# Weight sums of the FFN up-projection: bound on VectorE behind the subtraction two places ahead in the plan, where it was one

## The chip, the core and the metric

One core of a Trainium2 chip runs one inference step of a hybrid streaming encoder layer. The metric is the device time of one execution in microseconds (us).

## The reference

Two request groups share the weights: 256 prompt frames and 8 streams of 16 frames, together 384 rows of 2048. The part of the layer that the change touches is the feed-forward network at its end:

```python
h2 = rmsnorm(x, norm_ffn_g)
up = h2 @ w_up                          # 2048 x 11264: gate half, then up half, 5632 columns each
g_half = up[..., :D_FF]
u_half = up[..., D_FF:]
gc = causal_dwconv(concat([ffn_buf, g_half]), ffn_dw_w, ffn_dw_b)
x = x + (silu(gc) * u_half) @ w_down
```

Before it stand the combined input projection, the conformer convolution, the forgetting attention and the output projections, all in float32.

## The kernel before

Every weight goes to TensorE as a pair of halves. A DMA brings a tile of 2 x 128 rows by 512 columns (512 KB) into a slot; ScalarE (ACT) casts it to `hi` (L170), VectorE (DVE) subtracts `hi` from it to get `lo` (L171), and TensorE (PE) makes three matmuls for each product: `hi` with the high half of the activations, `lo` with that half, `hi` with their low half (L1180 to L1182 in the up-projection, L322 to L324 elsewhere). In the feed-forward part there are three pairs of `hi` and `lo`, used in turn, so the cast for a unit can only begin once TensorE is through with the unit three places ahead of it. The raw slots are seven, used in turn.

The feed-forward part is walked in eleven groups of 512 gate and 512 up columns, 0 to 10; after every second group the down-projection of those groups follows (after 8, of 8, 9 and 10). TensorE's order is fixed by hand. For a part of the 2048 rows (two quarters `q`; three of them in groups 3, 5, 7 and 9) the up-projection saves products by a scheme of Strassen's kind: it multiplies not only blocks of the weights but sums of blocks. For one quarter there are four blocks: `b11` and `b21` (gate columns, upper and lower rows) and `b12` and `b22` (up columns). The units, in TensorE's order, with the number of matmuls that read each:

| unit | weight that is split | VectorE's work on it | matmuls |
|---|---|---|---|
| b22 | the block itself | subtraction | 12 |
| t3 | `sums` = b22 + b12 | add, subtraction | 12 |
| t1 | b12 = b12 + b11, in its slot | add, subtraction | 6 |
| b11 | the block itself | subtraction | 12 |
| t2 | `sums` += b11 | add, subtraction | 6 |
| b21 | the block itself | subtraction | 12 |
| t4 | `sums` += b21 | add, subtraction | 6 |

The units `pu` and `pg` of the other quarters are plain blocks with 18 matmuls each. In a group with two mixed quarters one or more `pu` follow each `t1` or the last `t2`; in groups 3, 5, 7 and 9 the second and third quarter follow each other with no plain unit between them (b22 t3 t1 b11 t2, b22 t3 t1 b11 t2).

`planned_mixed` puts one function for each unit into `plan`; `ahead` calls them up to three units before TensorE needs them. A function loads what it needs, makes the add (L203, `add_to`) and then calls `split`, which records the cast and the subtraction. On VectorE and ScalarE a scheduler orders the instructions; the code binds some of them by an edge that sets an order on one engine and waits for nothing (`behind`). An add is bound behind the subtraction of the unit that was split last. Beside this work VectorE evacuates products (L1232 to L1261), turns blocks (L337), and makes the taps and products of the small convolution (L1151 to L1161).

Of the kernel before, what the change touches and what calls it, by code (L numbers as in the profile page):

```python
# [11 lines left out]
ALU = mybir.AluOpType  # L12
# [36 lines left out]
def hybrid_step(  # L49
# [41 lines left out]
    def f(ap):  # L91
        return ap.bitcast(F32)
# [3 lines left out]
    tt = nc.vector.tensor_tensor  # L96
# [8 lines left out]
    newest = {}  # L105

    def behind(d, name):
        tc.add_manual_dep(d.ins, name, mybir.DependencyInfo(
            mybir.DependencyClass.NoSync, mybir.DependencyReason.DATA), reason="queue")
# [35 lines left out]
    def fetch(srcs, by_row=False):  # L145
        slot = slots.pop(0)
        slots.append(slot)
        raw = wp.tile([P, 2, 512], F32, tag="raw", bufs=3, name="raw") if slot is None else slot
        o = 0
        for s in srcs:  # L150
            n = s.shape[-1]
            for k in ((0, 1), (1, 2)) if by_row else ((0, 2),):
                d = nc.sync.dma_start(raw[:, k[0]:k[1], o:o + n], s[:, k[0]:k[1], :])
                queued(d, len(plan) >= v_last)
            o += n
        return raw, o

    depth, ffn = [2], [False]
    pairs_more, splits = [], [0]

    def split(raw, o, by_row=False):
        n = splits[0] % depth[0] - 2
        splits[0] += 1
        if n >= 0:
            hi, lo = pairs_more[n]
        else:
            hi = wp.tile([P, 2, 512], F32R, tag="hi", bufs=2, name="hi")
            lo = wp.tile([P, 2, 512], F32R, tag="lo", bufs=2, name="lo")
        for k in (slice(0, 1), slice(1, 2)) if by_row else (slice(0, 2),):
            nc.scalar.copy(hi[:, k, :o], raw[:, k, :o])  # L170
            newest["lo"] = tt(lo[:, k, :o], raw[:, k, :o], f(hi[:, k, :o]), op=ALU.subtract).ins.name  # L171
        return hi, lo

    plan = []
# [1 line left out]
    def rows_of(w, k, c, n):  # L176
        return w[0, k * P:(k + 2) * P, c:c + n].rearrange("(k p) n -> p k n", p=P)
# [8 lines left out]
    def steps(g):  # L186
        mixed = mixed_of(g)
        pu, pg = ([(f"p{side}{h}", q) for q in range(4) if q not in mixed for h in range(2)] for side in "ug")
        n = len(pu) // 2 if g else 0
        top, low = [], []  # L190
        for i, q in enumerate(mixed):
            top += [(what, q) for what in ("b22", "t3", "t1")] + pu[i:min(i + 1, n)]
            top += [(what, q) for what in ("b11", "t2")]
            low += [[("b21", q), ("t4", q)]]
        if len(mixed) == 2:
            return top + pu[n:] + pg[:1] + low[0] + pg[1:2] + low[1] + pg[2:]
        return top + pu[n:] + low[0] + pg[:1] + low[1] + low[2] + pg[1:]

    def planned_mixed(w, c1, c2, g):
        held = {}  # L200

        def add_to(dst, a, b):
            behind(tt(dst, a, b, op=ALU.add), newest["lo"])  # L203

        def load(rows):
            return fetch([rows])[0]

        def add(fn):
            plan.append(lambda: split(fn(), 512))

        def single(name, k, c):
            held[name] = load(rows_of(w, k, c, 512))
            return held[name]

        def both(q):
            sums[q] = new_sum[0](q)
            add_to(sums[q], held["b22"][:], single("b12", 4 * q, c2)[:])
            return sums[q]

        def across(q):  # L220
            b = held["b12"][:]
            add_to(b, b, single("b11", 4 * q, c1)[:])
            return b

        def grown(q, name):
            add_to(sums[q], sums[q], held[name][:])
            return sums[q]

        make = {"b22": lambda q: single("b22", 4 * q + 2, c2), "t3": both, "t1": across,
                "b11": lambda q: held["b11"], "t2": lambda q: grown(q, "b11"),  # L230
                "b21": lambda q: single("b21", 4 * q + 2, c1), "t4": lambda q: grown(q, "b21")}
        for what, q in steps(g):
            if what[0] == "p":
                k, c = 4 * q + 2 * int(what[2]), {"u": c2, "g": c1}[what[1]]
                add(lambda k=k, c=c: load(rows_of(w, k, c, 512)))
            else:
                add(lambda what=what, q=q: make[what](q))
# [38 lines left out]
    def ahead(n):  # L276
        while plan and len(ready) < n:
            with tc.high_priority(offset=SPLIT_AHEAD):
                if x_left and (len(plan) - v_last) in range(3, 14, 2):
                    load_x(x_left.pop(0), 2)  # L280
                item = plan.pop(0)
                ready.append(item() if callable(item) else split(*fetch(item)))
# [80 lines left out]
    def natural(ap):  # L363
        return ap.rearrange("p (t i c) -> p i t c", t=NTT, i=4)
# [30 lines left out]
    with tc.manual_schedule(engines={ENG.SP, ENG.Activation, ENG.DVE}):  # L395
        nc.vector.memset(junk[:, 0:1], 0.0)
        nc.scalar.activation(junk[:, 1:2], junk[:, 0:1], AF.Identity)
        load_x(0, 1, nc.scalar)
        load_x(1, 1, nc.scalar)
        raws = [fetch(plan.pop(0), by_row=True)]  # L400
        raws.append(fetch(plan.pop(0)))
        load_x(2, 2)
        nc.scalar.dma_start(gm_row[:], norm_mix_g[0].rearrange("(c p) -> c p", p=P))
        warm = misc_tile()
        for i in range(WARM):
            mm(warm[:, :P], ident[:], ident[:], start=True, stop=True)
        pv = misc_tile()
        tr(pv[:, :16], gm_row[:], ident[:16, :16])
        nc.vector.tensor_copy(gm[:], pv[:, :16])
        x_chunk(0)  # L410
        for i in range(WARM_MID):
            mm(warm[:, :P], ident[:], ident[:], start=True, stop=True)
        x_chunk(1)
        for i in range(WARM_END):
            mm(warm[:, :P], ident[:], ident[:], start=True, stop=True)
        ready.append(split(*raws[0], by_row=True))
        ready.append(split(*raws[1]))
# [347 lines left out]
    def load_v(h):  # L765
# [14 lines left out]
                  k=kv[h // 4][:, :, :, h % 4, :]) for h in range(H)]  # L780
# [100 lines left out]
    for h in range(H):  # L881
        v = heads[h]["q"]
        hi, lo = (natural(aHL[h // 4][:, i, h % 4, :]) for i in range(2))
# [473 lines left out]
```

## Time and profile before

| | |
|---|---|
| median of 3 runs | 1980.43 us (1979.89 to 1980.8) |
| profiled execution: time, span | 1980.97 us, 1979.3 us |
| granted TensorE clock | 1.00 in every stretch |
| PE, PEld, DVE, ACT, POOL busy share | 99%, 83%, 66%, 45%, 13% |
| feed-forward part, from about | 910 us to the end |
| a period of two groups and their down-projection | 192.5 us |

Busy times are sums over instructions. A matmul of 512 columns has a record of 0.39 us, but the next begins 0.23 us after it, so TensorE loses more than its idle time shows when it has to wait: the record of the one before covers part of the wait.

### The profile page before, as it was taken

The page shows a single profiled execution, that of the slowest core. Times are in us where ns is not written, and L with a number is a line of the kernel's source. Part 1 is how long each engine was busy: PE and PEld are TensorE (multiplying, and loading weights), DVE is VectorE, ACT ScalarE, POOL GpSimd, SP SyncE. Part 2 cuts the span into 40 slices and gives each one's busy share as a digit, 9 for nine tenths or more (in the row PEclk, how much of TensorE's full clock was granted, in tenths as well). Part 3 has the DMA queues.
Part 4 walks back from the last instruction along what each step waited for, and adds up shares of the span by engine and source line. Part 5 has one row for each costly group of instructions (what it writes and reads, how often), then busy time and mean ns, then how long its engine had stood idle before and what let it go on. Part 6 is the DMA issues. An engine that isn't in the chain of part 4 may idle for free.

```text
span 1979.3 us, 24793 instructions
## 1 busy us (share of the span) xinstructions
PE 1957.6 (99%) x9230; PEld 1643.3 (83%) x9230; DVE 1301.2 (66%) x1715; ACT 898.6 (45%) x1310; POOL 260.0 (13%) x525
## 2 busy tenths in 40 slices
PE   9999999999999999999999999999999999999999
PEld 9999878888888888887888887888788878887887
DVE  4478889747465447457688648854885588558853
ACT  5433343555334423445455444553454345444541
POOL 1001121100000002011112200220022012201210
PEclk9999999999999999999999999999999999999999
DMA  6565776665344448767655675566567655756463
GB/s 185 157 170 161 225 238 201 203 186 156 114 131 122 128 133 273 236 210 233 200 168 180 203 181 154 183 209 169 162 190 207 167 176 181 209 149 191 157 232 113
DMA packets 194901, 358.21 MB, mean 181 GB/s; under 512 B 16386, under 2 KB 66557, under 8 KB 194771
## 3 DMA queue, kind: packets, MB, share of 16 engines
q1 hardware_dynamic: 172779, 272.78, 44.4%
q0 software_dynamic: 21680, 83.70, 15.2%
q8 instruction: 72, 1.18, 0.2%
q14 instruction: 50, 0.41, 0.1%
q10 hardware_dynamic: 320, 0.14, 0.0%
HBM read 301.78 MB, written 55.24 MB: 180 GB/s over the span
## 4 chain that ended last, share of the span: by engine, by line
PE 45%; DVE 3%; ACT 1%; issue 1%; POOL 0%; ACTq 0%; DVEq 0%
PE acc L1181 7%; PE acc L1182 6%; PE acc L1180 6%; PE acc L322 6%; PE acc L324 6%; PE acc L323 6%; PE misc L1181 2%; PE misc L1182 2%; PE misc L1180 2%; DVE lo L171 2%; ACT hi L170 1%; PE misc L322 1%; PE misc L324 1%; PE misc L323 1%; DVE rest L1233 0%
## 5 line engine op out<-in xcount | busy, mean ns | idle before, releaser
L171 DVE TENSOR_TENSOR lo<-raw,hi 128x1024 fp32r<-128x1024 f32 (+2 forms) x345 | 413.2, 1199 | 406.2 <-ACT hi L170 405.7
L170 ACT CAST hi<-raw 128x1024 fp32r<-128x1024 f32 (+2 forms) x345 | 354.6, 1030 | 605.9 <-PE acc L324 418.5
L322 PE MATMUL acc<-hi,hT 128*128 128x512 f32 (+1 forms) x704 | 270.4, 384 | 0.1
L323 PE MATMUL acc<-lo,hT 128*128 128x512 f32 (+1 forms) x704 | 266.1, 378 | 1.5 <-DVE lo L171 1.4
L324 PE MATMUL acc<-hi,hT 128*128 128x512 f32 (+1 forms) x704 | 265.6, 377 | 0.0
L171 DVE TENSOR_TENSOR lo<-rest,hi 128x1024 fp32r<-128x1024 f32 x136 | 165.3, 1221 | 110.2 <-ACT hi L170 109.7
L170 ACT CAST hi<-rest 128x1024 fp32r<-128x1024 f32 x136 | 142.0, 1048 | 125.8 <-PE acc L324 38.2
L322 PE MATMUL acc<-hi,act 128*128 128x512 f32 x484 | 188.3, 389 | 0.0
L323 PE MATMUL acc<-lo,act 128*128 128x512 f32 x484 | 188.3, 389 | 0.0
L324 PE MATMUL acc<-hi,act 128*128 128x512 f32 x484 | 188.3, 389 | 0.0
L323 PEld LDWEIGHTS acc<-lo,hT 128*128 128x128 f32 x704 | 132.3, 188 | 25.7 <-DVE lo L171 4.6
L588 DVE SCALAR_TENSOR_TENSOR ut<-ext,cw,ut 128x384 f32<-128x384 f32 x240 | 149.6, 623 | 5.5
L322 PEld LDWEIGHTS acc<-hi,hT 128*128 128x128 f32 x704 | 132.2, 188 | 24.1 <-issue 1.8
L324 PEld LDWEIGHTS acc<-hi,hT 128*128 128x128 f32 x704 | 132.2, 188 | 22.6
L1181 PE MATMUL acc<-lo,xg 128*128 128x512 f32 x384 | 149.6, 389 | 0.8 <-DVE lo L171 0.8
L1180 PE MATMUL acc<-hi,xg 128*128 128x512 f32 x384 | 149.5, 389 | 0.0
L1182 PE MATMUL acc<-hi,xg 128*128 128x512 f32 x384 | 149.4, 389 | 0.0
L170 ACT CAST hi<-sums 128x1024 fp32r<-128x1024 f32 x78 | 81.9, 1050 | 146.7 <-DVE sums L203 122.6
L1181 PE MATMUL acc<-lo,xm 128*128 128x512 f32 x340 | 134.6, 396 | 9.3 <-DVE lo L171 9.2
L1182 PE MATMUL acc<-hi,xm 128*128 128x512 f32 x340 | 132.4, 390 | 0.0
L1180 PE MATMUL acc<-hi,xm 128*128 128x512 f32 x340 | 132.4, 389 | 0.0
L342 POOL DMA_DIRECT2D turn<-block x124 | 69.2, 565 | 479.2 <-DVE block L337 470.4
(358 smaller groups left out, 3666.2 us busy)
## 6 DMA issues: line engine op xcount, KB each, us to landing
rest<-in_w_up_dram SPq DMA_DIRECT2D x97, 512.0 KB
raw<-in_w_in_dram SPq DMA_DIRECT2D x96, 512.0 KB
raw<-in_w_up_dram SPq DMA_DIRECT2D x79, 512.0 KB
raw<-in_w_down_dram SPq DMA_DIRECT2D x49, 512.0 KB
turn<-block POOLq DMA_DIRECT2D x120, 192.0 KB, 4.6
block<-turn POOLq DMA_DIRECT2D x30, 768.0 KB, 6.2
rest<-in_w_down_dram SPq DMA_DIRECT2D x39, 512.0 KB
raw<-in_w_in_dram SPq DMA_DIRECT2D x64, 256.0 KB
```

Source lines behind the costliest of these rows:

```text
L170: nc.scalar.copy(hi[:, k, :o], raw[:, k, :o])
L171: newest["lo"] = tt(lo[:, k, :o], raw[:, k, :o], f(hi[:, k, :o]), op=ALU.subtract).ins.name
L322: mm(o, ah[:, s], hi[:, kk, :n], start=st, stop=False)
L323: mm(o, ah[:, s], lo[:, kk, :n], start=False, stop=False)
L324: mm(o, al[:, s], hi[:, kk, :n], start=False, stop=sp)
L342: nc.gpsimd.dma_start(d[:, :, i, :].rearrange("j r n -> r j n"), src[32 * i:32 * i + 32, :].rearrange("r (j n) -> r j n", j=4))
L588: stt(o, v, wc, o, op0=ALU.mult, op1=ALU.add)
L1180: mm(o, ah, hi[:, kk, :], start=st, stop=False)
L1181: mm(o, ah, lo[:, kk, :], start=False, stop=False)
L1182: mm(o, al, hi[:, kk, :], start=False, stop=last[b] == (i, n))
```

## The change

The name of every subtraction is kept in a list in the order of the plan, and an add is bound behind the last but one of them instead of the last. Nothing else is edited.

```diff
-    pairs_more, splits = [], [0]
+    pairs_more, splits, halves = [], [0], []
...
-            newest["lo"] = tt(lo[:, k, :o], raw[:, k, :o], f(hi[:, k, :o]), op=ALU.subtract).ins.name
+            halves.append(tt(lo[:, k, :o], raw[:, k, :o], f(hi[:, k, :o]), op=ALU.subtract).ins.name)
...
         def add_to(dst, a, b):
-            behind(tt(dst, a, b, op=ALU.add), newest["lo"])
+            behind(tt(dst, a, b, op=ALU.add), halves[-2])
```

What the scheduler makes of it is shown by the order of the instructions in the two builds. TensorE's order is the same in both. Before the feed-forward part nothing moves on any engine. In it, VectorE, ScalarE, GpSimd and the DMA queue of SyncE are reordered; the number of instructions stays.

First place: VectorE in group 5, from the plain block b22 of the second quarter to the sum t1 of the third. `rest3_7742` in the first rows of the third quarter is its b22, `raw_11126` its b12 and `raw_11139` its b11; `rest2_7741` is the second quarter's b11. Before:

```order
L171 TENSOR_TENSOR lo3_6749<-sums_7738,hi3_6748 128x1024
L203 TENSOR_TENSOR rest1_7740<-rest1_7740,rest2_7741 128x1024
L171 TENSOR_TENSOR lo_11069<-rest1_7740,hi_11068 128x1024
L171 TENSOR_TENSOR lo_11085<-rest2_7741,hi_11084 128x1024
L203 TENSOR_TENSOR sums_7738<-sums_7738,rest2_7741 128x1024
L171 TENSOR_TENSOR lo_11111<-rest3_7742,hi_11110 128x1024
L171 TENSOR_TENSOR lo3_6749<-sums_7738,hi3_6748 128x1024
L203 TENSOR_TENSOR sums_7738<-rest3_7742,raw_11126 128x1024
L171 TENSOR_TENSOR lo_11130<-sums_7738,hi_11129 128x1024
L203 TENSOR_TENSOR raw_11126<-raw_11126,raw_11139 128x1024
L171 TENSOR_TENSOR lo_11157<-raw_11139,hi_11156 128x1024
L171 TENSOR_TENSOR lo3_6749<-raw_11126,hi3_6748 128x1024
```

After:

```order
L203 TENSOR_TENSOR rest1_7740<-rest1_7740,rest2_7741 128x1024
L171 TENSOR_TENSOR lo3_6749<-sums_7738,hi3_6748 128x1024
L171 TENSOR_TENSOR lo_11069<-rest1_7740,hi_11068 128x1024
L203 TENSOR_TENSOR sums_7738<-sums_7738,rest2_7741 128x1024
L171 TENSOR_TENSOR lo_11085<-rest2_7741,hi_11084 128x1024
L171 TENSOR_TENSOR lo3_6749<-sums_7738,hi3_6748 128x1024
L203 TENSOR_TENSOR sums_7738<-rest3_7742,raw_11126 128x1024
L171 TENSOR_TENSOR lo_11111<-rest3_7742,hi_11110 128x1024
L203 TENSOR_TENSOR raw_11126<-raw_11126,raw_11139 128x1024
L171 TENSOR_TENSOR lo_11130<-sums_7738,hi_11129 128x1024
L171 TENSOR_TENSOR lo3_6749<-raw_11126,hi3_6748 128x1024
```

Each add stands one subtraction earlier, and the subtractions now stand in TensorE's order: before, b22 of the third quarter stood ahead of t2 of the second, and b11 ahead of t1. ScalarE's casts are swapped back in the same way at these two spots.

Second place: VectorE in group 6 (two mixed quarters), around t1 of the second quarter (`rest3_7742`) and the plain unit that follows it in TensorE's order (`raw_11530`). Before:

```order
L203 TENSOR_TENSOR sums_7738<-rest2_7741,rest3_7742 128x1024
L171 TENSOR_TENSOR lo_11496<-sums_7738,hi_11495 128x1024
L203 TENSOR_TENSOR rest3_7742<-rest3_7742,raw_11506 128x1024
L171 TENSOR_TENSOR lo3_6749<-raw_11530,hi3_6748 128x1024
L171 TENSOR_TENSOR lo_11510<-rest3_7742,hi_11509 128x1024
L171 TENSOR_TENSOR lo_11552<-raw_11506,hi_11551 128x1024
```

After, where the row of the quarter's b22 (`rest2_7741`) now stands between the two adds:

```order
L203 TENSOR_TENSOR sums_7738<-rest2_7741,rest3_7742 128x1024
L171 TENSOR_TENSOR lo3_6749<-rest2_7741,hi3_6748 128x1024
L203 TENSOR_TENSOR rest3_7742<-rest3_7742,raw_11506 128x1024
L171 TENSOR_TENSOR lo_11496<-sums_7738,hi_11495 128x1024
L171 TENSOR_TENSOR lo_11510<-rest3_7742,hi_11509 128x1024
L171 TENSOR_TENSOR lo3_6749<-raw_11530,hi3_6748 128x1024
```

The subtraction of t1 moved ahead of that of the plain unit, and its add ahead of t3's subtraction. Groups 2, 4, 8 and 10 read alike.

Third place: VectorE in group 5, around t4 of the first quarter (the add of `rest0_7739` to `sums_7738`) and six instructions that evacuate products (L1232 to L1241). Before:

```order
L171 TENSOR_TENSOR lo_11203<-rest0_7739,hi_11202 128x1024
L1232 TENSOR_TENSOR rest0_7739<-misc_11059,rest0_7739 128x512
L203 TENSOR_TENSOR sums_7738<-sums_7738,rest0_7739 128x1024
L1233 SCALAR_TENSOR_TENSOR rest1_7740<-rest0_7739,nr2_6763,rest1_7740 128x512
L1236 SCALAR_TENSOR_TENSOR block_11214<-acc_11005,nr2_6763,rest1_7740 128x512
L1237 SCALAR_TENSOR_TENSOR block_11214<-acc_11005,nr2_6763,block_11214 128x512
L1244 SCALAR_TENSOR_TENSOR block_11214<-acc_11020,r2_6762,block_11214 128x512
L1241 SCALAR_TENSOR_TENSOR block_11214<-acc_10970,r2_6762,block_11214 128x512
L171 TENSOR_TENSOR lo_11220<-sums_7738,hi_11219 128x1024
```

After:

```order
L203 TENSOR_TENSOR sums_7738<-sums_7738,rest0_7739 128x1024
L171 TENSOR_TENSOR lo_11203<-rest0_7739,hi_11202 128x1024
L1232 TENSOR_TENSOR rest0_7739<-misc_11059,rest0_7739 128x512
L171 TENSOR_TENSOR lo_11220<-sums_7738,hi_11219 128x1024
L1233 SCALAR_TENSOR_TENSOR rest1_7740<-rest0_7739,nr2_6763,rest1_7740 128x512
L1236 SCALAR_TENSOR_TENSOR block_11214<-acc_11005,nr2_6763,rest1_7740 128x512
L1237 SCALAR_TENSOR_TENSOR block_11214<-acc_11005,nr2_6763,block_11214 128x512
L1244 SCALAR_TENSOR_TENSOR block_11214<-acc_11020,r2_6762,block_11214 128x512
L1241 SCALAR_TENSOR_TENSOR block_11214<-acc_10970,r2_6762,block_11214 128x512
```

The add went ahead of b21's subtraction, and t4's own subtraction ahead of five of the six evacuations.

## The prediction

> **What bounds the kernel now.** I read the page's first part, then who waited for whom on TensorE, then engine by engine the places where TensorE waits.
>
> ```profile
> PE 1957.6 (99%) x9230; PEld 1643.3 (83%) x9230; DVE 1301.2 (66%) x1715; ACT 898.6 (45%) x1310; POOL 260.0 (13%) x525
> ```
> ```profile
> PE acc L1181 <- DVE lo L171: 10.0, 16, 1.5
> PE misc L1181 <- DVE lo L171: 2.3, 4, 0.6
> ```
>
> TensorE is the bound, and its end is the kernel's end. All that a change on VectorE can give is TensorE's waiting. In the feed-forward part that is 12.3 us of idle time in 20 waits, all of them of L1181, the matmul with `lo`, for its subtraction. A wait costs more than its idle time. TensorE around the start of t2 of group 5's second quarter:
>
> ```profile
> 1388.90 0.39 PE L1182 MATMUL misc<-hi,xm 128*128 128x512 f32 x1
> 1389.12 0.39 PE L1180 MATMUL misc<-hi,xm 128*128 128x512 f32 x1
> 1390.09 0.50 PE L1181 MATMUL misc<-lo,xm 128*128 128x512 f32 x1 [0.58 <-DVE lo L171]
> 1390.43 0.40 PE L1182 MATMUL misc<-hi,xm 128*128 128x512 f32 x1
> ```
>
> The usual step is 0.23 us (1388.90 to 1389.12; 12 matmuls 2.71, 6 of them 1.35, 18 of them 4.06). Here it is 0.97, and the next one 0.34: lost are 0.74 + 0.11 = 0.85 us, the idle time and 0.27 more. So 20 waits lose 12.3 + 20 x 0.27 = 17.7 us. That is the most to be had, 0.9% of the time.
>
> The same view for the stretch from 883 to 1020 us (groups 0 and 1):
>
> ```profile
> PE acc L1181 <- DVE lo L171: 3.1, 3, 1.5
> ```
>
> These three lose 3.9 us. The other 17 have 12.3 - 3.1 = 9.2 us of idle time and lose 13.8 us: one in each of the five even groups from 2 on, three in each of 3, 5, 7 and 9.
>
> VectorE is the late one though it is busy for only 66%. Its subtractions wait for ScalarE's casts, and casts of sums wait for the adds:
>
> ```profile
> DVE lo L171 <- ACT hi L170: 568.9, 326, 4.9
> ACT hi L170 <- DVE sums L203: 122.6, 58, 2.9
> ```
>
> **The change, place by place.** No instruction is added or removed; 104 adds of 1.22 us move. First, group 5, before t2 of the second quarter, VectorE and then ScalarE:
>
> ```profile
> 1377.89 1.22 DVE L203 TENSOR_TENSOR sums<-rest,rest 128x1024 f32<-128x1024 f32 x1
> 1380.30 1.23 DVE L171 TENSOR_TENSOR lo<-sums,hi 128x1024 fp32r<-128x1024 f32 x1 [1.19 <-ACT hi L170]
> 1381.45 1.22 DVE L203 TENSOR_TENSOR rest<-rest,rest 128x1024 f32<-128x1024 f32 x1
> 1383.86 2.36 DVE L171 TENSOR_TENSOR lo<-rest,hi 128x1024 fp32r<-128x1024 f32 x2 [1.19 <-ACT hi L170]
> 1386.13 1.22 DVE L203 TENSOR_TENSOR sums<-sums,rest 128x1024 f32<-128x1024 f32 x1
> 1387.67 1.23 DVE L171 TENSOR_TENSOR lo<-rest,hi 128x1024 fp32r<-128x1024 f32 x1 [0.32 <-ACT hi L170]
> 1388.82 1.22 DVE L171 TENSOR_TENSOR lo<-sums,hi 128x1024 fp32r<-128x1024 f32 x1
> 1389.95 1.22 DVE L203 TENSOR_TENSOR sums<-rest,raw 128x1024 f32<-128x1024 f32 x1
> ```
> ```profile
> 1382.78 2.00 ACT L170 CAST hi<-rest 128x1024 fp32r<-128x1024 f32 x2 [2.50 <-DVE rest L203]
> 1386.59 1.05 ACT L170 CAST hi<-rest 128x1024 fp32r<-128x1024 f32 x1 [1.82 <-PE acc L1182]
> 1387.55 1.05 ACT L170 CAST hi<-sums 128x1024 fp32r<-128x1024 f32 x1
> ```
>
> Each sum goes through add, cast, subtraction with VectorE idle for 1.19 us during the cast, 3.5 us in a row, three times a quarter. Instructions on VectorE start 1.14 us apart when nothing holds them. Where no plain unit of 4.06 us stands between, TensorE (10.8 us a quarter) is faster than that chain (adds of t3 at 1377.89 and 1389.95: 12.1 us). t2's matmuls begin at 1389.12 and want its subtraction one step later, 1389.35; it is done at 1390.04. Its cast had also stood behind one of the next quarter, which waited until 1386.59 for its pair. Counted back by the units' lengths, b11 began at 1386.4 (its own `lo` wanted at 1386.63), t1 at 1385.0, t3 at 1382.3.
>
> With the new order: t1's add fills the idle 1.19 us ahead of 1380.30; its subtraction follows t3's, at 1381.45 instead of 1383.86. Then t2's add, 1382.6 to 1383.8; b11's subtraction, whose pair is free at 1382.3 and cast by 1383.5, 1383.75 to 1385.0 (it was done at 1386.22); t2's cast when its pair is free, with t3's last matmul, 1385.0 to 1386.05; t2's subtraction done at 1387.3, 2 us early.
>
> The second wait there is t1 of the third quarter (chain of waits):
>
> ```profile
> 1394.36 1.06 ACT hi L170
> 1395.45 2.37 DVE lo L171 x2
> 1397.86 0.50 PE acc L1181
> ```
>
> b11's subtraction goes first and t1's second. On from above: t3's add 1387.2, b22's subtraction 1388.35, t1's add 1389.5, t3's subtraction 1390.6 (cast from 1389.2, when its pair is free), t1's cast 1390.75, subtraction 1391.85 to 1393.1. Without the first wait TensorE wants it at 1389.12 + 1.35 + 2.71 + 2.71 + 0.23 = 1396.1. Both waits go.
>
> Third, t4 of the first quarter:
>
> ```profile
> 1403.14 1.23 DVE L171 TENSOR_TENSOR lo<-rest,hi 128x1024 fp32r<-128x1024 f32 x1 [0.65 <-ACT hi L170]
> 1406.02 0.74 DVE L1233 SCALAR_TENSOR_TENSOR rest<-rest,nr,rest 128x512 f32<-128x512 f32 x1
> 1407.47 0.74 DVE L1237 SCALAR_TENSOR_TENSOR block<-acc,nr,block 128x512 f32<-128x512 f32 x1
> 1408.78 0.74 DVE L1241 SCALAR_TENSOR_TENSOR block<-acc,r,block 128x512 f32<-128x512 f32 x1
> 1409.44 1.22 DVE L171 TENSOR_TENSOR lo<-sums,hi 128x1024 fp32r<-128x1024 f32 x1
> 1410.71 0.50 PE L1181 MATMUL acc<-lo,xm 128*128 128x512 f32 x1 [0.30 <-DVE lo L171]
> ```
>
> The five evacuations from 1406.02 to 1409.5 stood ahead of its subtraction. Now it goes ahead of them, and they begin one subtraction (1.14 us) later but without the add (1.13) that was ahead. Without the two waits before, TensorE ends the third quarter at 1389.12 + 12.2 = 1401.3; b21's subtraction is then done at about 1402.3, L1232 at 1402.9, t4's at 1404.1 (wanted 6.8 us after 1401.3), the five evacuations of 0.7 us at 1407.5, and the next plain unit's subtraction at 1408.7, wanted at 1401.3 + 4.06 + 2.71 + 1.35 + 0.23 = 1409.65: 0.9 us to spare. The PSUM bank that t4 writes is free when L1237 is done, 1406.1, also in time. The wait goes.
>
> Fourth, group 6's t1 (VectorE, and TensorE's wait):
>
> ```profile
> 1444.06 1.23 DVE L171 TENSOR_TENSOR lo<-sums,hi 128x1024 fp32r<-128x1024 f32 x1 [1.19 <-ACT hi L170]
> 1447.31 1.23 DVE L171 TENSOR_TENSOR lo<-raw,hi 128x1024 fp32r<-128x1024 f32 x1 [0.89 <-ACT hi L170]
> 1448.45 1.22 DVE L171 TENSOR_TENSOR lo<-rest,hi 128x1024 fp32r<-128x1024 f32 x1
> 1449.72 0.50 PE L1181 MATMUL acc<-lo,xm 128*128 128x512 f32 x1 [0.64 <-DVE lo L171]
> ```
>
> Its add now runs in the 1.19 us ahead of 1444.06, its subtraction at 1445.2 to 1446.4, wanted at 1448.9. The plain unit keeps its 1447.31.
>
> So all 17 repeating waits go: **-13.8 us**.
>
> Groups 0 and 1 are crowded with the evacuation of the output projection:
>
> ```profile
> 910.58 1.23 DVE L171 TENSOR_TENSOR lo<-raw,hi 128x1024 fp32r<-128x1024 f32 x1 [0.90 <-ACT hi L170]
> 911.72 1.22 DVE L203 TENSOR_TENSOR sums<-raw 128x1024 f32<-128x1024 f32 x1
> 912.86 1.88 DVE L1058 TENSOR_TENSOR y<-acc,y 128x512 f32<-128x512 f32 x3
> 914.70 1.22 DVE L171 TENSOR_TENSOR lo<-sums,hi 128x1024 fp32r<-128x1024 f32 x1
> 917.61 2.32 DVE L171 TENSOR_TENSOR lo<-raw,hi 128x1024 fp32r<-128x1024 f32 x2
> ```
>
> After, t1's add, two evacuations and t1's subtraction stand between 911.7 and t3's subtraction: 1.14 + 2 x 0.6 + 1.14 = 3.5, so it begins at 915.2 instead of 914.70 and may miss its matmul by 0.2 us, by 1 if t1's rows land late. Bounds for these three waits: nothing saved to 3.9. I take 1 us left: **-2.9 us**.
>
> What may be late next: an add now holds a subtraction behind it, and in the even groups one tap of the small convolution stands ahead of t2's. The trace has no such order. Bounds: nothing, where VectorE idles 1.19 us (as at 1380.30), to one wait of 0.85 us in each group, 9.4 us. I take 0.5, near the lower end, since the places above have 0.9 us and more to spare: **+0.5 us**.
>
> GpSimd's queue and SyncE's are reordered too. Rows of weights are issued as slots come free, and an add that runs earlier frees its slot earlier; I cost that at nothing.
>
> Sum: -13.8 - 2.9 + 0.5 = -16.2 us, from 1980.97 us of the profiled execution to 1964.8. That run stands 0.54 us above the median, so the median goes from 1980.43 to **1964.2 us**.
>
> **Rivals.**
>
> *The ring of three pairs is the limit.* The casts that begin the late stretches waited for TensorE (1386.59 above, 1394.36, both behind L1182), and an earlier add frees no pair. [...] Against: t2's own pair was free at 1385.0, 2.5 us before its cast began. If it holds, only groups 0 and 1 gain: 1980.4 - 2.9 = 1977.5 us.
>
> *Half.* The swapped subtractions (t2, t1) come right, but the evacuations or the taps, now elsewhere between them, make new waits of the old size in half of the places: 1980.4 - 8.1 = 1972.3 us.
>
> *Slower: adds hold up plain blocks.* If t1's subtraction stayed at 1383.86, t2's add would push b11's from 1386.22 to 1387.36, 0.73 us behind TensorE's 1386.63, in place of a wait that had 0.41 to spare. At 0.73 each, 24 such places eat the 17.7 us; t2 and t4 have 52. With all of them and nothing gained on the way: 1980.4 - 17.7 + 52 x 0.73 = 2000 us. Against: t1's chain moves too.
>
> **How the numbers follow.** The sum as it stands, 1962 to 1966.5: 0.68. Half (1966.5 to 1975.5): 0.18. The ring, or no effect: 0.08. Slower: 0.06. The runs before spread by 0.9 us, so 0.2% (4 us) is about what can be told from no change. Faster by more than that: 0.68 + 0.18 + 0.01 of the ring's upper end = 0.87; within: 0.07; slower: 0.06. The likeliest case's own range is 1962 to 1966.5; 1962 is all 17.7 us and a little. The range for 8 in 10 reaches up through most of the half: 1961.8 to 1972.
>
> **What would show it.** TensorE's waits for `lo` in the feed-forward part fall from 20 to under 5; no wait at t2, t1 and t4 of groups 3, 5, 7 and 9; VectorE's idle time behind ScalarE's casts falls, while its busy time stays near 1301 us; TensorE's busy time stays near 1958 us. A period of 192.5 us becomes 189.3 (four waits of 0.85, 0.91, 0.57, 0.91 less). Waits at b11 or at plain units in their place would show the slower rival, unchanged waits the ring. The prediction is wrong if the chain through ScalarE, not VectorE's order, keeps t1 and t2 late, or if the taps ahead of t2 wait for GpSimd.

## The result and the profile after

| | before | after |
|---|---|---|
| median (runs) | 1980.47 us (6: 1979.37 to 1980.8) | 1965.49 us (6: 1964.4 to 1966.94) |
| profiled execution: time, span | 1980.97 us, 1979.3 us | 1965.24 us, 1963.5 us |
| ratio, 95% interval | | 0.9926, 0.9914 to 0.9938 |

The change takes 15 us off, 0.74%; 1964.2 was forecast, from 1961.8 to 1972. The page's first lines of after:

```profile
PE 1952.4 (99%) x9230; PEld 1647.6 (84%) x9230; DVE 1300.8 (66%) x1715; ACT 903.2 (46%) x1310; POOL 255.8 (13%) x525
```

The work on each engine is the same. PE's busy time fell by 5.2 us although nothing was taken from it: the record of the matmul ahead of a wait, and that of the waiting one (0.50 where 0.39 is usual), hold part of the wait. Who waited for whom on TensorE, after (us in total, times, longest; two rows that read the same in before are left out):

```profile
PE acc L1180 <- DVE block L1237: 2.4, 1, 2.4
PE acc L1181 <- DVE lo L171: 0.6, 2, 0.3
PE acc L323 <- DVE lo L171: 0.4, 2, 0.3
```

Of the 20 waits of L1181 two are left, 0.6 us, and both are in groups 0 and 1. All 17 repeating ones are gone. The row of L1237 is new. The same view over all engines, one row of before and then three of after:

```profile
ACT hi L170 <- PE acc L1182: 69.7, 53, 2.4
```
```profile
DVE lo L171 <- ACT hi L170: 546.7, 324, 4.4
ACT hi L170 <- PE acc L1182: 120.2, 111, 3.0
ACT hi L170 <- DVE sums L203: 7.0, 7, 2.5
```

The casts' waits for the adds into `sums` (122.6 us in 58 waits before) are 7.0 us in 7 now. Casts wait for TensorE instead, which means for their pair, twice as often: they are ready early, and wait where waiting costs nothing, but for one place in group 0 (below). VectorE around t2 of group 5's second quarter, after (start, duration; in brackets the idle time before it and its releaser):

```profile
1374.20 1.23 DVE L171 TENSOR_TENSOR lo<-sums,hi 128x1024 fp32r<-128x1024 f32 x1 [0.37 <-ACT hi L170]
1375.56 1.22 DVE L171 TENSOR_TENSOR lo<-rest,hi 128x1024 fp32r<-128x1024 f32 x1
1376.70 1.22 DVE L203 TENSOR_TENSOR sums<-sums,rest 128x1024 f32<-128x1024 f32 x1
1378.27 1.23 DVE L171 TENSOR_TENSOR lo<-rest,hi 128x1024 fp32r<-128x1024 f32 x1 [0.36 <-ACT hi L170]
1381.00 1.22 DVE L171 TENSOR_TENSOR lo<-sums,hi 128x1024 fp32r<-128x1024 f32 x1 [1.50 <-ACT hi L170]
1382.14 1.22 DVE L203 TENSOR_TENSOR sums<-rest,raw 128x1024 f32<-128x1024 f32 x1
1383.27 1.22 DVE L171 TENSOR_TENSOR lo<-rest,hi 128x1024 fp32r<-128x1024 f32 x1
```

From the top: t3's and t1's subtractions, t2's add, b11's subtraction, t2's (at 1381.00), t3's add of the third quarter, b22's. The order is the plan's. Before, the 1.19 us of a cast stood idle in front of t3's and t1's subtraction; now there is 0.37 and nothing, and t2's cast, not its add, is what its subtraction waits for.

To account for all of the time I add up, from the first matmul of the feed-forward part, what each step from one matmul's start to the next exceeds the usual 0.226 us by (2.71 us for 12), over all steps above 0.26 ("lost"). The part's length less this sum is nearly the same for every kernel of this study with three pairs, 1046.3 to 1047.5 us: TensorE's losses there are nearly the whole difference, 13.5 of the 14.2 us between these two.

| kernel (profiled execution) | ahead of the part | the part | lost in it | part less lost |
|---|---|---|---|---|
| before | 913.4 | 1065.9 | 18.8 | 1047.1 |
| after | 911.9 | 1051.7 | 5.3 | 1046.4 |

The part is 14.2 us shorter. The other 1.5 us of the span lie ahead of it, where no instruction moved; the executions below have 911.9 to 914.0 there, so that is not the change's.

### The profile page after: what moved, and what is told of

Same layout as the page of the kernel before. It is cut to its first block, busy times and chain, and to the rows that moved or that the text cites. A ratio compares the mean times of both kernels' runs of the same rounds, so it can differ in the third digit from the quotient of the medians.

```text
span 1963.5 us, 24810 instructions
## 1 busy us (share of the span) xinstructions
PE 1952.4 (99%) x9230; PEld 1647.6 (84%) x9230; DVE 1300.8 (66%) x1715; ACT 903.2 (46%) x1310; POOL 255.8 (13%) x525
## 5 line engine op out<-in xcount | busy, mean ns | idle before, releaser
L323 PE MATMUL acc<-lo,hT 128*128 128x512 f32 (+1 forms) x704 | 265.5, 377 | 0.4 <-DVE lo L171 0.4
L323 PE MATMUL acc<-lo,act 128*128 128x512 f32 x484 | 188.3, 389 | 0.0
L323 PEld LDWEIGHTS acc<-lo,hT 128*128 128x128 f32 x704 | 132.3, 188 | 22.9 <-DVE lo L171 1.6
L1181 PE MATMUL acc<-lo,xg 128*128 128x512 f32 x384 | 149.8, 390 | 0.3 <-DVE lo L171 0.3
L1181 PE MATMUL acc<-lo,xm 128*128 128x512 f32 x340 | 132.4, 389 | 0.3 <-DVE lo L171 0.3
L171 DVE TENSOR_TENSOR lo<-sums,hi 128x1024 fp32r<-128x1024 f32 x78 | 95.0, 1217 | 33.8 <-ACT hi L170 33.6
```

What stands on the lines that cost most here:

```text
L171: halves.append(tt(lo[:, k, :o], raw[:, k, :o], f(hi[:, k, :o]), op=ALU.subtract).ins.name)
L323: mm(o, ah[:, s], lo[:, kk, :n], start=False, stop=False)
L1181: mm(o, ah, lo[:, kk, :], start=False, stop=False)
```

## The experiments

Their names: `t1`, `t3` and so on as in the table of units; a "pair" is one `hi` and one `lo`. Three questions were open: was it the earlier add or the order of the subtractions that it brought; what is the new wait of group 0; and do the pairs set a limit.

### Order without the earlier add, and the earlier add without the order

The first, on the kernel after:

```diff
-            behind(tt(dst, a, b, op=ALU.add), halves[-2])
+            behind(tt(dst, a, b, op=ALU.add), halves[-1])
...
-            halves.append(tt(lo[:, k, :o], raw[:, k, :o], f(hi[:, k, :o]), op=ALU.subtract).ins.name)
+            d = tt(lo[:, k, :o], raw[:, k, :o], f(hi[:, k, :o]), op=ALU.subtract)
+            if ffn[0]:
+                behind(d, halves[-1])
+            halves.append(d.ins.name)
```

> Adds bound behind the last subtraction as in the kernel before, but every subtraction of the feed-forward part bound behind the subtraction of the unit ahead of it in the plan, so that VectorE takes them in TensorE's order. Theory A (an add behind the last subtraction makes add, cast, subtraction one chain of 3.5 us in which VectorE idles 1.19 us; only the earlier add breaks it): the five waits of the even groups go (the plain unit no longer stands ahead of t1), but in groups 3, 5, 7 and 9 t2 of the second quarter stays late by about 0.2 to 0.5 us and t1 of the third by 1: 1971 to 1978 us. Rival C (the earlier add does nothing by itself, all was the order of the subtractions): all 17 waits go, 1963 to 1967 us. Rival (forced order is worse than the scheduler's): above 1981 us.

Measured: 1984.15 us, ratio to before 1.0018 (1.0009 to 1.0027): slower than before, and lost are 22.2 us. TensorE's waits from 883 us on:

```profile
PE acc L1184 <- DVE lo L171: 8.1, 17, 0.8
PE misc L1184 <- DVE lo L171: 4.5, 10, 0.8
```

27 waits instead of 20. VectorE in group 5, b22 of the second quarter to b22 of the third:

```profile
1378.53 1.23 DVE L171 TENSOR_TENSOR lo<-rest,hi 128x1024 fp32r<-128x1024 f32 x1 [0.65 <-ACT hi L170]
1379.67 1.22 DVE L206 TENSOR_TENSOR sums<-rest,rest 128x1024 f32<-128x1024 f32 x1
1382.09 1.23 DVE L171 TENSOR_TENSOR lo<-sums,hi 128x1024 fp32r<-128x1024 f32 x1 [1.19 <-ACT hi L170]
1383.23 1.22 DVE L206 TENSOR_TENSOR rest<-rest,rest 128x1024 f32<-128x1024 f32 x1
1385.64 2.36 DVE L171 TENSOR_TENSOR lo<-rest,hi 128x1024 fp32r<-128x1024 f32 x2 [1.19 <-ACT hi L170]
1387.92 1.22 DVE L206 TENSOR_TENSOR sums<-sums,rest 128x1024 f32<-128x1024 f32 x1
1390.40 1.23 DVE L171 TENSOR_TENSOR lo<-sums,hi 128x1024 fp32r<-128x1024 f32 x1 [1.27 <-ACT hi L170]
1391.55 1.22 DVE L171 TENSOR_TENSOR lo<-rest,hi 128x1024 fp32r<-128x1024 f32 x1
```

With nothing to put between a late add and its own subtraction, VectorE idles three times a quarter, and a quarter takes it 13.0 us (1378.53 to 1391.55) where TensorE needs 10.8. So VectorE's order alone is worth less than nothing, and rival C falls. My own number was too low: I had not counted t3 of the third quarter (0.6 us lost) and t2 of the third (0.7) becoming late too, and the five waits of the even groups, which were to go, stay with 0.7 us lost each. The swaps of the kernel before had been filling idle time.

The edit binds VectorE only. On ScalarE the casts stayed swapped; group 5, b22 of the third quarter and behind it t2 of the second:

```profile
1388.38 1.05 ACT L170 CAST hi<-rest 128x1024 fp32r<-128x1024 f32 x1 [1.82 <-PE acc L1185]
1389.33 1.04 ACT L170 CAST hi<-sums 128x1024 fp32r<-128x1024 f32 x1
```

t2's add ended at 1389.14, so its cast lost about 0.2 us to the swap, of a wait of 0.39: by this estimate the wait would be shorter with the casts in order, but not gone. In group 6 t1's cast began 0.8 us after its add had ended, behind the plain unit's, and its wait is 0.44 us: there the casts' order may be what was left. No run has the order on both engines without the early add.

The second keeps the early adds and puts the two swaps back, on VectorE alone:

```diff
-            halves.append(tt(lo[:, k, :o], raw[:, k, :o], f(hi[:, k, :o]), op=ALU.subtract).ins.name)
+            d = tt(lo[:, k, :o], raw[:, k, :o], f(hi[:, k, :o]), op=ALU.subtract)
+            if swap and swap[0] == splits[0] - 1:
+                behind(halves_d[-1], d.ins.name)
+                swap.pop(0)
+            halves.append(d.ins.name)
+            halves_d.append(d)
```

where `swap` is filled for b22 and b11 of the third quarter in groups 3, 5, 7 and 9.

> The changed kernel with its early adds, but in groups 3, 5, 7 and 9 the two swaps of the kernel before are put back on VectorE: t2 of the second quarter is subtracted behind b22 of the third, and t1 of the third behind its b11. Theory A alone (only the earlier add matters): as the changed kernel, 1965 to 1966 us. Rival C (only the order matters): all eight waits of these two places return, 0.85 to 0.91 us each, 7 us: 1972.5 us. Both (my theory): t2 waits for b22's pair, which TensorE frees only when t1 of the second quarter is through, so four waits of about 0.85 us return; b11's pair is freed when b22 of the third quarter is through, about 2 us before t1 is wanted, so t1 loses 0 to 0.5: 1969 to 1971 us.

Measured: 1973.9 us, ratio 0.9964 (0.9951 to 0.9976). Both waits are back in all four groups, 0.91 us each: eight times 0.91 is 7.3 us, and 12.8 are lost in all against 5.3. That is rival C's number; my own 1969 to 1971 was wrong for t1. The subtractions of b22 and t2 on VectorE, the cast of b22 on ScalarE, and TensorE (lines are shifted by 10 there):

```profile
1385.37 1.23 DVE L171 TENSOR_TENSOR lo<-rest,hi 128x1024 fp32r<-128x1024 f32 x1 [2.85 <-ACT hi L170]
1386.51 1.22 DVE L171 TENSOR_TENSOR lo<-sums,hi 128x1024 fp32r<-128x1024 f32 x1
```
```profile
1382.93 1.05 ACT L170 CAST hi<-sums 128x1024 fp32r<-128x1024 f32 x1 [1.67 <-PE acc L1192]
1384.29 1.05 ACT L170 CAST hi<-rest 128x1024 fp32r<-128x1024 f32 x1 [0.31 <-PE acc L1192]
```
```profile
1387.79 0.50 PE L1191 MATMUL misc<-lo,xm 128*128 128x512 f32 x1 [0.63 <-DVE lo L171]
```

t2 was cast at 1383.98, but stood behind b22's subtraction, whose cast could begin only when TensorE let go of the pair of t1, at about 1384.26. From there it is 0.03 + 1.05 + 0.03 + 1.14 + 1.22 = 3.5 us to the end of t2's subtraction, while b11's matmuls last 2.71 and `lo` is wanted 0.23 later: 0.5 us too late by this count, 0.63 by the trace. At t1 of the third quarter it is the same sum with b11's pair and t3's 2.71 us; I had seen a slack of 2 us there that does not exist.

The two together, for the eight places in groups 3, 5, 7 and 9: neither half does the work. Early adds without the order leave these places as they were (0.85 and 0.91 us before, 0.91 and 0.91 here); VectorE's order without early adds idles VectorE. The change gains there because the early add is what lets VectorE run in TensorE's order without idling. For t4 and for the even groups the two were not taken apart. Nor does a run part the change from the new order of GpSimd's and SyncE's queues; none of the 17 waits was for them.

### Which adds

Only t1 and t2 early (`add_to` gets a number, and t3 and t4 pass 1):

```diff
-        def add_to(dst, a, b):
-            behind(tt(dst, a, b, op=ALU.add), halves[-2])
+        def add_to(dst, a, b, n=2):
+            behind(tt(dst, a, b, op=ALU.add), halves[-n])
...
-            add_to(sums[q], held["b22"][:], single("b12", 4 * q, c2)[:])
+            add_to(sums[q], held["b22"][:], single("b12", 4 * q, c2)[:], 1)
...
-            add_to(sums[q], sums[q], held[name][:])
+            add_to(sums[q], sums[q], held[name][:], 2 if name == "b11" else 1)
```

> The changed kernel, but only the adds of t1 and t2 are bound behind the last but one subtraction; those of t3 and t4 behind the last, as before. The order of the subtractions of groups 3, 5, 7 and 9 is still that of the plan up to b21; t4's add and subtraction fall behind b21's and the evacuations again. My theory (VectorE has 8 instructions a quarter, 9.1 us of TensorE's 10.8; with t1's add in the 1.19 us of t3's cast nothing is late): the waits at t2 of the second quarter and t1 of the third stay away; t4 of the first quarter in group 5 is subtracted at about 1403.7 against 1403.0 wanted, so four waits lose 0.7 to 0.9 each: 1968 to 1970 us. Rival (any add behind the last subtraction brings the chain back): also the waits at t2 and t1, 7 us more, 1973 to 1977 us.

Measured: 1971.52 us, ratio 0.9957 (0.9942 to 0.9972). TensorE's waits from 883 us on:

```profile
PE acc L1180 <- ACT xg L1072: 6.3, 1, 6.3
PE acc L1181 <- DVE lo L171: 1.5, 5, 0.3
```

As expected t1 and t2 stay in time, and t4 of groups 3, 5, 7 and 9 waits again: 0.30 us each, 0.58 lost, less than I gave. The miss is a wait of 6.3 us in group 0 and the slow steps behind it, 8.0 us lost together where after loses 4.1 at its pause. It was released by the cast that makes `xg`, the activations of the plain units, on ScalarE, whose own queue had waited 3.6 us for turned blocks to land:

```profile
ACT block L1069 <- DMA block<-turn: 3.6, 1, 3.6
```

That is a second way in which group 0 can stop TensorE, with another releaser than L1237.

Only t3 and t4 early (the same edit, with 1 for t1 and t2):

> The counterpart: only the adds of t3 and t4 are bound behind the last but one subtraction, those of t1 and t2 behind the last. Theory: t1's and t2's chains are kept, each with 1.19 us of idle VectorE: t1 of the third quarter stands behind b11 again (four waits of 0.9), t2 of the second is late by 0.5 to 0.8 (four), t1 of the even groups loses 0.7 (five), t4 gains: 1973 to 1979 us. Rival (t3's add is the one that counts): 1966 to 1968 us.

Measured: 1969.47 us, ratio 0.9946 (0.9932 to 0.9961). My range missed, and the rival, that t3's add counts, comes nearer. t1 of the third quarter loses 0.73 us in four groups (0.9 was expected) and t3 of the third 0.46, but t2, t4 and the five even groups have no wait, and group 0 has no pause. In the even groups t3's early add was enough: in group 6 t1's subtraction (1439.90) is back ahead of the plain unit's (1441.05). So either half of the adds removes 13 of the 17 waits, this half with four smaller ones in exchange; both are needed for all.

### How far ahead

Three places instead of two (`halves[-3]`), and no binding at all (`tt(dst, a, b, op=ALU.add)` by itself):

> The changed kernel with adds bound behind the last but two subtractions instead of the last but one. Theory (two places are enough, since nothing of the 17 waits is left; what remains is group 0): within 2 us of the changed kernel, 1963.5 to 1967.5 us. Rival (an add whose rows have not landed stands at the head of VectorE's queue): waits of TensorE at units whose subtraction stands behind it, 1970 us and more.

> The changed kernel with the adds bound to nothing: the scheduler's order has them up to nine units ahead. Theory (the bound had kept adds near their place; too early, they hold up subtractions when rows land late, and the slots of rows are held as before): same or slower than the changed kernel, 1965 to 1972 us. Rival (binding was only ever a cost): 1961 to 1964 us.

Measured: 1966.85 us, ratio 0.9935 (0.9918 to 0.9952), and 1975.74 us, 0.9976 (0.9967 to 0.9985). Three places are as good as two: no wait behind group 0, and in group 0 a pause of 2.8 us, released by `xg` as in the kernel with only t1 and t2 early. Unbound adds go up to nine units ahead, and that costs 10 us against after. VectorE in group 9 of the unbound kernel:

```profile
1761.24 1.23 DVE L203 TENSOR_TENSOR rest<-rest,rest 128x1024 f32<-128x1024 f32 x1 [3.08 <-DMA rest<-in_w_up_dram]
1762.38 1.22 DVE L171 TENSOR_TENSOR lo<-raw,hi 128x1024 fp32r<-128x1024 f32 x1
```

and TensorE:

```profile
1763.65 0.79 PE L1181 MATMUL acc<-lo,xm 128*128 128x512 f32 x1 [2.17 <-DVE lo L171]
```

The add of t1 of the third quarter waits 3.08 us for rows at the head of VectorE's queue; behind it stands b22 of the second, which TensorE wants first. My range ended at 1972; the direction and the reason were right.

### The new wait of group 0

After, at the first plain gate unit of group 0: VectorE, ScalarE, TensorE.

```profile
951.87 1.23 DVE L171 TENSOR_TENSOR lo<-sums,hi 128x1024 fp32r<-128x1024 f32 x1 [1.01 <-ACT hi L170]
953.01 0.75 DVE L1237 SCALAR_TENSOR_TENSOR block<-acc,nr,block 128x512 f32<-128x512 f32 x1
```
```profile
950.79 1.05 ACT L170 CAST hi<-sums 128x1024 fp32r<-128x1024 f32 x1 [2.35 <-PE acc L1182]
951.74 0.72 ACT L1235 ACTIVATE block<-rest,r 128x512 f32<-128x512 f32 x1
```
```profile
953.81 0.80 PE L1180 MATMUL acc<-hi,xg 128*128 128x512 f32 x1 [2.38 <-DVE block L1237]
```

TensorE wants the PSUM bank (its accumulator) that holds the product `p5`, which L1237 frees. L1237 needs the block that L1235 scales on ScalarE, and L1235 stood there behind the cast of t4, which waited 2.35 us for its pair. Before, the row of the same L1235 was

```profile
948.60 0.72 ACT L1235 ACTIVATE block<-rest,r 128x512 f32<-128x512 f32 x1
```

ahead of that cast. An early add lets its cast go to the head of ScalarE's queue too soon. Behind the pause one step is 0.59 us and six are 0.43 instead of 0.23: about 1.6 us more.

Two tests. The first takes group 0 back (`halves[-2 if g else -1]`):

> The changed kernel, but in group 0 the adds are bound behind the last subtraction, as in the kernel before. If what happens in group 0 is only of its own making: its old waits return (t1 of both quarters, t3 of the second: 3.2 us), its new ones go (t3 0.6 us; 4.5 us at the bank of L1237): 1.3 to 1.9 us less than the changed kernel, about 1963.8 us, 0.9916; all other groups as in the changed kernel. If the gain of the other groups hung on work shifted in group 0: above 1965.5 us.

Measured: 1964.42 us, ratio 0.9918 (0.9904 to 0.9932). 1.1 us less than after (1.3 to 1.9 expected); 3.8 us are lost instead of 5.3: the pause is gone, the old waits are back, and the rest is as in after. What the other groups gain does not hang on group 0.

The second puts the scaling ahead of the cast, and only that:

```diff
-    pairs_more, splits, halves = [], [0], []
+    pairs_more, splits, halves, first = [], [0], [], []
...
-            nc.scalar.copy(hi[:, k, :o], raw[:, k, :o])
+            cast = nc.scalar.copy(hi[:, k, :o], raw[:, k, :o])
+            if first:
+                behind(cast, first.pop())
...
         def grown(q, name):
+            if (g, q, name) == (0, 0, "b21"):
+                first.append(newest["scaled"])
...
-            nc.scalar.activation(u[:, 0], e0, AF.Identity, scale=scale[0])
+            newest["scaled"] = nc.scalar.activation(u[:, 0], e0, AF.Identity, scale=scale[0]).ins.name
```

> The changed kernel, and in group 0 the cast of the first quarter's t4 is bound behind ScalarE's scaling of the first two row blocks' product (L1235 of the kernel before), which it stood ahead of. Theory (the new 2.4 us wait of group 0 is ScalarE's queue: the cast of t4 waited there for its pair, L1235 behind it, VectorE's L1237 behind that, and TensorE for the bank that L1237 frees; and the seven slow steps of 0.43 us are the clock granted after that pause): TensorE's wait near 954 us goes, and with it 2.9 us of pause and 1.6 us of slow steps: about 4.5 us less than the changed kernel, 1961.0 us, 0.990 of the kernel before. Rival 1, the slow steps have another cause and stay: 1962.6 us. Rival 2, the bank comes late for another reason (L1236 or VectorE's own order): the wait stays, 1965.5 us.

Measured: 1961.64 us (1961.45 to 1963.33), ratio 0.9906 (0.9892 to 0.9919). The waits of TensorE from 883 us on:

```profile
PE acc L1185 <- DVE lo L173: 0.6, 2, 0.3
PE acc L1184 <- ACT acc L1063: 0.2, 1, 0.2
```

Lost are 1.7 us instead of 5.3, and the time is 3.9 us less than that of after. I had expected 4.5, but the pause and the slow steps overlap in one step; together they lose 4.1. The same stretch of time, after and then this kernel (columns: length, busy time of PE, PEld, DVE, ACT, POOL, granted clock, DMA share, GB/s):

```profile
953.80:957.00 3.20, 3.19 (x8) 2.52 (x9) 2.42 (x4) 0.69 (x1) 0.49 (x1) 0.50 0.02 5
```
```profile
953.80:957.00 3.20, 3.20 (x16) 2.65 (x15) 2.52 (x4) 0.91 (x1) 0.00 (x0) 1.00 0.20 74
```

Half the clock, half the matmuls (8 against 16) for 3.2 us. Without the pause the slow steps are gone as well, so rival 1 falls, and rival 2 with it. Both kernels once more side by side on one chip:

> The changed kernel once more, as the one to set the next beside on the same chip. Theory: 1965.5 us within 1 us, with the pause of 2.4 us near 954 us and a half clock behind it again. Rival (the pause comes from rows that land late by chance): no pause in this execution, 1961 to 1963 us.

> The cast of t4 of group 0 behind L1235, once more beside the changed kernel. Theory: 3.5 to 4.5 us less than it, 1961 to 1962 us, no pause of TensorE over 1 us after 880 us. Rival (the 3.9 us between the two were the difference of two chips): within 2 us of it.

Measured: 1966.55 us (1964.68 to 1967.52), ratio 0.9927 (0.9913 to 0.994), and 1963.32 us (1962.17 to 1963.79), ratio 0.9911 (0.9898 to 0.9925). The pause is there again in the first (2.4 us, L1237) and not in the second. The difference, 3.2 us, is a little under the 3.5 expected, and the second time lies 1.3 us above its range; the two traces' losses differ by 4.1 (5.5 and 1.4), and 1.1 us of that is taken back ahead of the feed-forward part (912.9 and 914.0), where nothing differs. The kernel with the scaling first is the fastest of the study.

### The pairs

> The changed kernel with two pairs of hi and lo in the feed-forward part instead of three. The ring from its other side: with two, a cast begins when TensorE starts the unit before, and cast and subtraction need 0.03 + 1.05 + 0.04 + 1.22 = 2.34 us; a unit of 6 matmuls lasts 1.35 and the lo matmul is wanted 0.23 later, so each of the 78 units behind a t1, t2 or t4 is late by 0.8 and loses about 1 us: 75 us and more where the evacuations come between, 2040 to 2080 us. If the pairs were no limit at all: as the changed kernel, 1965 us.

The edit is one number, `SPARE = 0`. One run: 2052.61 us. TensorE's waits from 883 us on:

```profile
PE acc L1181 <- DVE lo L171: 46.5, 69, 0.9
PE misc L1181 <- DVE lo L171: 10.5, 14, 0.8
```

83 waits, most of them 0.76 us of idle time and 1.1 lost; 89.6 us are lost in all. Each of the 78 units behind a t1, t2 or t4 loses some of it. With two pairs the ring is the bound, at the places and of the size that the count gives. The 83 waits here come from too few buffers; the 17 repeating waits of the kernel before did not: they went without another buffer. A fourth pair was not tried.

## Why the prediction was right, and where not

**The bound and what it can give.** Right: 18.8 us were lost in the feed-forward part (17.7 by the rule of idle time and 0.27).

**The 17 repeating waits, -13.8 us.** The mechanism was right at all four places: none of the waits is left, and the period fell from 192.5 to 189.04 us (189.3 forecast). At these units 13.9 us had been lost; with small steps elsewhere 14.4 went (18.8 less the 4.4 of groups 0 and 1). The slack was right too. t2's subtraction (the row of 1381.00 above) ends at 1382.22, and t1's of the third quarter at 1388.06 (the first row here); TensorE takes them at the times of the other two,

```profile
1386.83 1.23 DVE L171 TENSOR_TENSOR lo<-raw,hi 128x1024 fp32r<-128x1024 f32 x1
```
```profile
1383.97 0.39 PE L1181 MATMUL misc<-lo,xm 128*128 128x512 f32 x1
...
1390.77 0.39 PE L1181 MATMUL acc<-lo,xm 128*128 128x512 f32 x1
```

which is 1.8 and 2.7 us later; 2 and 3 were forecast.

**Groups 0 and 1, -2.9 us.** This term was mis-sized. They lost 4.4 us before and lose 5.3 after, +0.9 instead of -2.9. I looked for waits for `lo` there, and t3's came about as feared (0.32 us of idle time, 0.61 lost; 0.2 to 1 was given), the last one shrank from 0.77 us to 0.29. What I did not see is a wait of another kind: L1237 and its bank, which I had worked through for group 5 only, where it is done at 1400.97 and in time. In group 0 the evacuation passes through ScalarE behind a cast that waits for a pair. Both experiments on group 0 show it; with the scaling put first, 1.7 us are lost in place of 4.4, -2.7, which is nearly the term.

**New waits, +0.5 us.** None behind group 0. From group 2 on the subtractions of t2, t3 and t4 end 1.3 us or more before TensorE takes them, so no tap held up t2.

**The sum.** -14.4 + 0.9 = -13.5 us against -16.2. The median fell by 15.0 and came within 1.3 us of the forecast all the same, partly by luck. In the profiled executions 0.7 us more went from the part than the losses show, and the part ahead of it, where nothing moved, was 1.5 us shorter, 1.0 of it by fewer waits of L323 (0.4 us of idle time against 1.4). By the traces the change itself is worth 13.5 (the losses) to 14.2 us (the part's length); the second measurement of the changed kernel gave 13.8.

**The rivals.** The ring did not hold here; that a pair's release times the casts was right, though, and it is why the swaps cost what they cost. "Half" happened at one place out of the many, in group 0. Slower did not happen: with the bound three places ahead there was still none of it, and only without a bound did adds hold up blocks, then for rows that had not landed.

**The signs.** VectorE's busy time stayed (1300.8); its idle time behind casts fell from 568.9 to 546.7 us; PE's busy time did not stay at 1958 but fell to 1952.4, for the reason above.

## What to carry to other kernels

Where one engine feeds another through a third (add, cast, subtraction), put each link one item ahead of the item it belongs to, so that the engine has other work in the gap; keep the consumer's order, and check by experiment that neither alone would do (1984.15 us with the order alone, 1973.9 with the early add alone, 1965.49 with both). In this kernel the link was the add. Two places ahead were enough here and three gave no more (1966.85 us); with no bound (1975.74 us) the instruction stood at the head of its queue before its data had landed, 3.08 us in the place shown. When casts get earlier, look at everything that stands behind them on their engine, at the ends of the loop as well as in its middle.

## What the runs showed that was not expected

A pause of TensorE cost more than its length in some of these kernels. In after, TensorE's pause of 2.38 us ended at 953.81 us, and the granted clock was 0.50 from 953.59 to 957.00; the pause and the slow steps lost 4.1 us together. In the kernel with the swaps the half clock came later behind a pause of the same length (2.4 us, ended at about 954.8): the granted clock was 0.97 from 954.70 to 956.40 and 0.51 from 956.40 to 959.80. With the pauses of 2.17 and 2.6 us in the unbound kernel it was 0.50 from 1763.60 to 1765.00 and 0.51 from 948.20 to 951.20. With the one of 6.3 us, where only t1 and t2 were early, it was 0.51 from 949.80 to 953.00, and 0.94 over 900 to 960 us, where after has 0.97. With the one of 2.8 us, with the bound three places ahead, it was 1.00 over 900 to 960 us. Two stretches of after, then two of that kernel (columns as above, the granted clock last but two):

```profile
950.17:953.59 3.42, 1.26 (x6) 0.72 (x4) 2.41 (x3) 2.24 (x3) 0.00 (x0) 1.00 0.50 149
953.59:957.00 3.41, 3.19 (x8) 2.52 (x9) 2.62 (x5) 0.69 (x1) 0.49 (x1) 0.50 0.02 5
```
```profile
943.00:946.50 3.50, 0.69 (x4) 0.23 (x2) 1.37 (x3) 2.60 (x5) 0.00 (x0) 1.00 0.97 360
946.50:950.00 3.50, 3.48 (x15) 2.70 (x16) 2.05 (x4) 2.22 (x5) 0.56 (x1) 1.00 0.96 338
```

What decides whether the clock falls with a pause, and when, these runs do not show: the pause of 2.8 us had no half clock, the shorter ones of 2.17 and 2.38 us had it.
